# Silu and SSM-branch tiles: PSUM copied out by ScalarE, the product on GpSimd; y tiles loaded first in the GLU stage

## Chip, cores and metric

The kernel runs on one core of a Trainium2 chip. The metric is the device time of one execution in microseconds (us). Times and rows below come from the runs of the kernel before and from one execution of it that the hardware profiler recorded.

## What is computed

One step of a hybrid encoder layer (D_MODEL 1024) on two token streams: a prompt of 1024 tokens and a sample of 32 tokens with a cache of 512. Everything is fp32. Cut to what the change touches:

```python
h = rms_norm(x, g_norm) * (1.0 + scale) + shift
z = h @ w_in
u, zs, q, k, v, za, qi, ki, wi, gm = split(z)
ys, hr, hi = ssm_scan(u, ...)                 # 32 groups of 16 channels, 64 complex states
ys = gelu(ys)
ys = ys * sigmoid(ys @ w_glu + b_glu)
ys = ys * silu(zs)
o  = sparse_attention(q, k, v, top-k keys by relu(qi . ki) weighted with wi)
ya = o * silu(za)
g_s, g_a = split(gm)
merged = sigmoid(g_s) * (ys @ w_ps) + sigmoid(g_a) * (ya @ w_pa)
x_new = x + gate * (merged @ w_o)             # then a final rms_norm
```

Here silu(x) = x * sigmoid(x), and the kernel gets it as (1 + tanh(x/2)) * x with the factor 1/2 taken up elsewhere. The sigmoid of the gates is made from a tanh in the same way.

## The kernel before

The two streams are put side by side: NT = 1056 columns (1024 + 32), cut into three column groups of G3 = 352. Features lie on the 128 partitions.

Each fp32 product is three fp32r matmuls (`mm3`, lines 271 to 273): high weights by high data, high weights by low data, low weights by high data. So each weight tile is split into `wh`, a cast of `raw` (line 259 on ScalarE, line 263 in pieces on GpSimd), and `wl = raw - wh` (line 264). The data are split into names that end in H and L.

The dense products are jobs in one queue, `Z`: u and zs tiles, the indexer's ki and qi0 to qi3, glu0 to glu3, gates g0 to g15, K/V/Q of the heads, za0 to za3 (silu of za), m0 to m7 (`psjob`, ys @ w_ps). A job has three column groups. A group is 3 x kt matmuls of 352 columns (kt = 8 for inputs of 1024 features, 4 for 512) into one PSUM bank: pool "z" (tile `pz`) has two banks; while nothing else uses them, halves of two larger tiles (`pss`) serve as well. A function `ev(n, ps)` empties a bank. The weights of the next job are split, and those of the one after it loaded, while the first column group of a job runs. `heng` and `leng` name the engines that make `wh` and `wl`.

The stages in order: modulation, norm and u (to about 90 us); SSM chains with zs, gates and ki between them (to about 245); the GLU stage (to about 305); indexer scores (318 to 405); 32 bisection rounds for the top-k threshold on VectorE and ScalarE, with K/V/Q and gates on TensorE (to 555); the marks of the chosen keys on VectorE, with za0 to za3 on TensorE (555 to 602); attention in four head pairs (608 to 893), m0 to m7 beside the last pair (815 to 905); then the merge and the output. TensorE's, VectorE's and ScalarE's orders are written by hand in most stages, GpSimd's and SyncE's (the DMA queue) are set by the tile scheduler. Every engine works through its own queue in order.

Names in the steps: `yD` is the GELU'd SSM output in DRAM, stored from `Yq` (line 991); `yg` its four tiles loaded again (line 1124), split into `ygH` (ScalarE, line 70) and `ygL` (line 73), the data of the glu jobs. `zsD` and `ztD` hold zs and its tanh; `gate_tile` loads them as `z2`, `t2` and forms the silu factor on VectorE (line 1090), `gate_y` multiplies it by yg (line 1095). `qis` are the parts of qi that VectorE and ScalarE take from its banks (lines 1067 to 1070). `cki` is the cached indexer keys. `th` (buffers "sth") is a tanh of one column group, `zt` a silu tile on its way to DRAM, `tg` in `psjob` (in the trace `tgl`) the tanh of a gate tile loaded from DRAM, `m1` (in the trace `m`) its product with ys @ w_ps, which is read again in the merge after 906 us. `PH` and `PL` are the halves of the attention weights.

Of the kernel before, what the change touches and what calls it, by code (L numbers as in the profile page):

```python
# [12 lines left out]
ALU = mybir.AluOpType  # L13
# [29 lines left out]
C_U, C_ZS, C_Q, C_K, C_V, C_ZA, C_QI, C_KI, C_GM = 0, 512, 1024, 1536, 2048, 2560, 3072, 3584, 3656  # L43
# [15 lines left out]
def body(nc, tc, I, O, dbg=None):  # L59
    ctx = ExitStack()  # L60
    dbg = dbg or (lambda name, ap: None)
    I = {k: v for k, v in I.items()}
    te, ve, se, ge, sp = nc.tensor, nc.vector, nc.scalar, nc.gpsimd, nc.sync

    def f32(ap):
        return ap.bitcast(F32)

    def split(h, l, src, heng, leng):
        if heng is se:
            se.copy(h, src)  # L70
        else:
            heng.tensor_copy(h, src)
        leng.tensor_sub(l, src, f32(h))  # L73
# [14 lines left out]
    def ps_x(tag, bufs, w=512):  # L88
        t = phase[1].tile([128, w], F32, tag=tag, bufs=bufs, name="ps" + tag)
        return t  # L90
# [14 lines left out]
    def ps_s(n="pss"):  # L105
        return ps_x("s", 2, 1024)
# [15 lines left out]
    def load_rows(xt, g, r, n, eng):  # L122
# [3 lines left out]
        if k < n:  # L126
# [30 lines left out]
                            op0=ALU.add, op1=ALU.mult)  # L157
# [163 lines left out]
    now, ve = ve, Later(ve, todo)  # L321
# [149 lines left out]
    for k in range(7):  # L471
        n = 1 << k
# [39 lines left out]
    ve = now  # L512
# [29 lines left out]
    ns = lambda n: slice(n * G3, (n + 1) * G3)  # L542
# [145 lines left out]
    ztD = [dram.tile([128, NT], F32, name=f"ztD{q}") for q in range(4)]  # L688
    zaD = [dram.tile([128, NT], F32, name=f"zaD{q}") for q in range(4)]

    def silu_job(name, c0, dst, heng, leng, th_dst=None):

        def begin():
            zt = stg.tile([128, NT], F32, tag="stg", name="zt")
            zth = stg.tile([128, NT], F32, name="zth", tag="zth", bufs=1) if th_dst is not None else None

            def ev(n, ps):
                if th_dst is not None:
                    se.activation(zth[:, ns(n)], ps, AF.Tanh, scale=0.5)
                    se.copy(zt[:, ns(n)], ps)  # L700
                else:
                    th = stg.tile([128, G3], F32, tag="sth", name="th")
                    se.activation(th, ps, AF.Tanh, scale=0.5)
                    ve.scalar_tensor_tensor(zt[:, ns(n)], th, 1.0, ps, op0=ALU.add, op1=ALU.mult)
                if n == 2:
                    sp.dma_start(dst, zt)
                    if th_dst is not None:
                        sp.dma_start(th_dst, zth)
            return ev
        return Job(name, wcol(c0), begin, heng=heng, leng=leng)  # L710

    def gate_job(f, heng, leng):
        def begin():
            tg = stg.tile([128, NT], F32, tag="stg", name="tg")

            def ev(n, ps):
                se.activation(tg[:, ns(n)], ps, AF.Tanh, scale=0.5)  # L717
                if n == 2:
                    sp.dma_start(thD[f], tg)
            return ev  # L720
        return Job(f"g{f}", wcol(C_GM + 128 * f), begin, heng=heng, leng=leng)
# [53 lines left out]
    for t in START.split():  # L775
# [6 lines left out]
        else:  # L782
            n = t.rstrip("0123456789")
            STEP[n](*(int(c) for c in t[len(n):]))
        if t == "wl00":
            ssm_shifts()
    ssm_consts()
    sp.dma_start(uD[0], uP[0])
    sp.dma_start(uD[1], uP[1])
    Z.add(*(silu_job(f"zs{q}", C_ZS + 128 * q, zsD[q], se, ge, ztD[q]) for q in range(4)),  # L790
          *(gate_job(f, se, ve) for f in range(NS)))
    while todo:
# [265 lines left out]
    cki = kp.tile([128, 4, 2, 64], F32)  # L1058
    QS = {}

    def qijob(j):
        def begin():
            qs = QS[j] = [kp.tile([128, NT], F32R, name=f"qis{e}", bufs=2) for e in range(2)]

            def ev(n, ps):
                c = ns(n)
                se.copy(qs[0][0:64, c], ps[0:64])
                se.copy(qs[1][64:128, c], ps[64:128])
                ve.tensor_sub(qs[0][64:128, c], ps[0:64], f32(qs[0][0:64, c]))
                ve.tensor_sub(qs[1][0:64, c], ps[64:128], f32(qs[1][64:128, c]))  # L1070
            return ev
        return Job(f"qi{j}", wcol(C_QI + 128 * j), begin, heng=se, leng=ve)
# [7 lines left out]
    def tok(t):  # L1080
        return ((t[:, 0:1024].rearrange("p (c s) -> p c s", s=8), slice(0, 128)),
                (t[:, 1024:NT].rearrange("p (c s) -> p c s", s=8), slice(129, 133)))
# [3 lines left out]
    def gate_tile(q):  # L1086
        z2, t2 = (gp.tile([128, NT], F32, name=n, bufs=b) for n, b in (("z2", 2), ("t2", 1)))
        sp.dma_start(z2, zsD[q])
        sp.dma_start(t2, ztD[q])
        ve.scalar_tensor_tensor(z2, t2, 1.0, z2, op0=ALU.add, op1=ALU.mult)  # L1090
        Z2.append(z2)

    def gate_y(q):
        for v_, c in tok(Z2[q]):
            ve.tensor_mul(v_, v_, yg[q][:, c])

    def glu_job(q):
        def begin():
            z2 = Z2[q]

            def ev(n, ps):
                c = ns(n)
                th = stg.tile([128, G3], F32, tag="sth", name="th")
                se.activation(th, ps, AF.Tanh, scale=0.25, bias=bglu[:, q:q + 1])
                ve.scalar_tensor_tensor(z2[:, c], th, 1.0, z2[:, c], op0=ALU.add, op1=ALU.mult)
                yo = [gp.tile([128, G3], F32R, name=f"yo{h}", bufs=3) for h in range(2)]
                split(yo[0], yo[1], z2[:, c], se, ge)
                for h in range(2):
                    sp.dma_start(ysD[h][q][:, c], f32(yo[h]))
                if n == 2 and q < 2:  # L1110
                    gate_tile(q + 2)
                    gate_y(q + 2)
            return ev
        return Job(f"glu{q}", w_glu[:, 128 * q:128 * q + 128], begin, kt=4, heng=se, leng=ve,
                   rhs=lambda n, k: (ygH[k][:, ns(n)], ygL[k][:, ns(n)]))

    for q in range(2):
        gate_tile(q)
    ckd = I["cache_kidx"].rearrange("a b (k p) d -> p (a b k) d", p=128)
    for hf_ in range(2):  # L1120
        sp.dma_start(cki[:, :, hf_], ckd)
    for q in range(4):
        yg.append(gp.tile([128, 8, NCH], F32, name=f"yg{q}").rearrange("p s c -> p c s"))
        sp.dma_start(yg[q].rearrange("p c s -> p s c"), yD[q])
# [1 line left out]
            split(h_, l_, yg[q][:, c], se, (ge, ve)[(YS >> q) & 1])  # L1126
    w_glu = I["w_glu"].rearrange("o d e -> (o d) e")
    for q in range(2):
        gate_y(q)
    Z.add(*(glu_job(q) for q in range(4)), qijob(1), *(gate_job(f, se, ve) for f in range(NS, NI - 1)))  # L1130
    Z.add(qijob(2), qijob(3), gate_job(NI - 1, se, ve), hold=True)
    Z.until("glu3")
# [49 lines left out]
    for k in range(9):  # L1182
        n = 128 if k < 8 else 32
# [16 lines left out]
    for j in range(4):  # L1200
# [3 lines left out]
        for i in range(2, 9):  # L1204
            t0, m, k0, nk = (128 * i, 128, 0, 128 * (i + 1)) if i < 8 else (1024, 32, 1024, 544)
            for e in range(2):
                h = 2 * j + e
                ps = ps_s()
                for a in range(0, nk, 512):
                    b = min(nk, a + 512)  # L1210
# [7 lines left out]
                else:  # L1218
                    ve.scalar_tensor_tensor(sco[i][:m, :nk], rl[:m, :nk], w, sco[i][:m, :nk],  # L1219
                                            op0=ALU.mult, op1=ALU.add)  # L1220
# [150 lines left out]
    class Soft:  # L1371

        def products(self, m, nk, mask, lhsT, rhs, np_=0):
            self.m, self.nk, self.mask, self.np_ = m, nk, mask, np_
            self.P = at2.tile([128, 1024], F32, name="Sm", bufs=SM)
            self.S = []
            for a in range(0, nk, 512):
                c = slice(a, min(nk, a + 512))
                S = ps_x("s", 3)[:m, 0:c.stop - a]
                self.S.append((c, S))  # L1380
                for t, r in enumerate(rhs):
                    te.matmul(S, lhsT, r[:, c], start=t == 0, stop=t == len(rhs) - 1)  # L1382
# [172 lines left out]
    def q0_end():  # L1555
# [3 lines left out]
        X.heads()  # L1559
    X.qjob.end = q0_end  # L1560
    Z.add(X.kjob, X.vjob, X.qjob, *(gate_job(f, ge, ge) for f in range(NI, 16)),
          *(silu_job(f"za{q}", C_ZA + 128 * q, zaD[q], se, ge) for q in range(4)))
    m1, PB = [], []

    def ps_branch():
# [7 lines left out]
    def psjob(f):  # L1573
        def begin():
            m1.append(late["fin"].tile([128, NT], F32, name="m1", tag="mm", bufs=8))
            tg = stg.tile([128, NT], F32, name="tgl", tag="stg")
            sp.dma_start(tg, thD[f])

            def ev(n, ps):
                ve.scalar_tensor_tensor(m1[f][:, ns(n)], tg[:, ns(n)], 1.0, ps, op0=ALU.add, op1=ALU.mult)  # L1580
            return ev
        return Job(f"m{f}", I["w_ps"].rearrange("o d e -> (o d) e")[:, 128 * f:128 * f + 128], begin, kt=4,
                   heng=se, leng=ge, rhs=lambda n, k: (PB[0][k, n], PB[1][k, n]))
# [95 lines left out]
    for k in range(len(seq) + 3):  # L1679
        it = at(k)  # L1680
        if k in first:
            p, begin = first[k]
# [10 lines left out]
        f = FA[p][e_] + FF * (it.i + 1 if it else 5)  # L1693
# [77 lines left out]
    for f in range(8):  # L1771
        wh, wl = wsplit(w_pa[:, 128 * f:128 * f + 128], 4, 128)
        tg = stg.tile([128, NT], F32, name="tgl", tag="stg")
        sp.dma_start(tg, thD[8 + f])
        for n in range(3):
            ps = ps_x("m", 4)
# [63 lines left out]
    for rows in ((0, 1, 2), (8,), (3,), (4,), (5,), (6,), (LAST,)):  # L1840
        xts = {}
        for hcol in range(2):
            for i in rows:
                n = 128 if i < 8 else 32
# [5 lines left out]
                for b_, c in enumerate(cols):  # L1850
                    ps = products(i, n, hcol, c)
# [4 lines left out]
                    if len(cols) == 2 and b_ == 0:  # L1856
                        ve.tensor_scalar(ss2[:n, 0, i:i + 1], ss2[:n, 0, i:i + 1], ss2[:n, 1, i:i + 1], None,
                                         op0=ALU.add)
# [53 lines left out]
```

## Time and profile before

| | us |
|---|---|
| three runs | 1049.63, 1050.88, 1049.40 |
| median | 1049.63 |
| the profiled execution's own time | 1053.21 |
| its span in the profile | 1051.4 |
| TensorE matmul busy | 999.1 (95%) |
| VectorE busy | 768.1 (73%) |
| ScalarE busy | 542.0 (52%) |
| GpSimd busy | 250.5 (24%) |

PE is TensorE's matmuls, PEld its weight loads, DVE is VectorE, ACT ScalarE, POOL GpSimd, SP SyncE, which issues nearly all DMAs. [...] In a row of the timeline the brackets say how long the engine stood idle before it and what ended that.

### The profile page before, as it was taken

What the parts mean: (1) busy time and instruction counts of PE and PEld (TensorE: products, weight loads), DVE (VectorE), ACT (ScalarE), POOL (GpSimd) and SP (SyncE); (2) the same over time, 40 slices, a digit from 0 to 9 for tenths busy, and PEclk for the clock granted to TensorE, in tenths of its full rate; (3) what the DMA queues carried; (4) which work ended last, traced back from release to release, by engine and by line L of the source; (5) the groups of instructions that cost most, each with busy time, mean ns of one, the idle gap of its engine ahead of it and who ended that gap; (6) DMA issues with size and microseconds to landing.
All of it is one profiled execution on the core that took longest, in us unless ns stands there. A gap on an engine that the chain in (4) does not pass through costs nothing.

```text
span 1051.4 us, 17200 instructions
## 1 busy us (share of the span) xinstructions
PE 999.1 (95%) x6194; PEld 929.9 (88%) x6194; DVE 768.1 (73%) x1756; ACT 542.0 (52%) x1164; POOL 250.5 (24%) x467
## 2 busy tenths in 40 slices
PE   5899999999899999998998999999999999999997
PEld 3799999999788989998998998899898988998786
DVE  4569898994776879988889846756658776786534
ACT  3542345544545656768994346655566555443111
POOL 4102400000240013333313532333233131340000
PEclk9899999999899999998998999999999999999999
DMA  9922632328483222223232341242124632754311
GB/s 309 272 69 83 185 123 63 94 72 243 158 267 101 61 61 81 79 84 92 82 103 82 104 141 53 63 132 70 59 86 126 203 93 75 268 164 139 128 63 60
DMA packets 125329, 126.00 MB, mean 120 GB/s; under 512 B 14400, under 2 KB 104980, under 8 KB 125244
## 3 DMA queue, kind: packets, MB, share of 16 engines
q1 hardware_dynamic: 124864, 124.59, 38.4%
q8 instruction: 49, 0.80, 0.3%
q14 instruction: 36, 0.29, 0.1%
q10 hardware_dynamic: 220, 0.28, 0.1%
q0 software_dynamic: 160, 0.03, 0.0%
HBM read 87.81 MB, written 36.50 MB: 118 GB/s over the span
## 4 chain that ended last, share of the span: by engine, by line
PE 66%; DVE 11%; ACT 10%; issue 5%; DMA 5%; SPq 1%; POOL 1%; ACTq 0%; POOLq 0%; DVEq 0%
PE pz L271 10%; PE pz L272 10%; PE pz L273 10%; ACT junkb L1546 5%; PE pss L1382 3%; PE psm L1881 3%; PE psm L1882 3%; PE psm L1883 3%; DMA wm<-in_w_mod 2%; PE pss L271 2%; PE pss L273 2%; DVE junk L1548 2%; PE pt L1475 2%; PE pss L272 2%; PE pspo L1494 2%
## 5 line engine op out<-in xcount | busy, mean ns | idle before, releaser
L271 PE MATMUL pz<-hH,wh 128*128 128x352 f32 (+1 forms) x776 | 260.1, 335 | 0.3 <-DVE qis L1070 0.2
L273 PE MATMUL pz<-hH,wl 128*128 128x352 f32 (+1 forms) x776 | 250.7, 323 | 0.0
L272 PE MATMUL pz<-hL,wh 128*128 128x352 f32 (+1 forms) x776 | 250.7, 323 | 0.0
L264 POOL TENSOR_TENSOR wl<-raw,wh 128x256 fp32r<-128x256 f32 (+1 forms) x184 | 133.7, 754 | 118.6 <-ACT wh L259 118.3
L271 PEld LDWEIGHTS pz<-hH,wh 128*128 128x128 f32 (+1 forms) x776 | 145.0, 187 | 4.2 <-issue 0.8
L272 PEld LDWEIGHTS pz<-hL,wh 128*128 128x128 f32 (+1 forms) x776 | 145.1, 187 | 1.5
L273 PEld LDWEIGHTS pz<-hH,wl 128*128 128x128 f32 (+1 forms) x776 | 144.9, 187 | 0.4
L1546 ACT ACTIVATE junkb<-sco,thr 128x896 bf16<-128x896 f32 (+3 forms) x128 | 103.5, 809 | 30.8 <-DVE thr L1611 20.7
L271 PE MATMUL pss<-hH,wh 128*128 128x352 f32 x304 | 103.8, 341 | 9.9 <-ACT tg L717 6.4
L272 PE MATMUL pss<-hL,wh 128*128 128x352 f32 x304 | 101.5, 334 | 0.3 <-DVE hL L73 0.2
L273 PE MATMUL pss<-hH,wl 128*128 128x352 f32 x304 | 101.3, 333 | 0.4 <-POOL wl L264 0.4
L1548 DVE TENSOR_SCALAR_CACHE_REDUCE junk<-sco,thr 128x1024 bf16<-128x1024 f32 (+2 forms) x96 | 96.9, 1010 | 2.3
L263 POOL CAST wh<-raw 128x256 fp32r<-128x256 f32 x88 | 34.7, 434 | 185.1 <-PE pz L272 169.3
L271 PEld LDWEIGHTS pss<-hH,wh 128*128 128x128 f32 x304 | 59.9, 197 | 13.9 <-POOL wh L263 5.2
L1478 DVE TENSOR_TENSOR PL<-pt,PH 128x512 fp32r<-128x512 f32 (+2 forms) x96 | 50.4, 553 | 27.7 <-ACT PH L1477 26.6
L1477 ACT CAST PH<-pt 128x512 fp32r<-128x512 f32 (+2 forms) x96 | 43.0, 482 | 42.9 <-PE pt L1475 39.6
L272 PEld LDWEIGHTS pss<-hL,wh 128*128 128x128 f32 x304 | 60.0, 197 | 0.8 <-DVE hL L73 0.8
L273 PEld LDWEIGHTS pss<-hH,wl 128*128 128x128 f32 x304 | 59.7, 196 | 0.9 <-POOL wl L264 0.9
L1219 DVE SCALAR_TENSOR_TENSOR sco<-rl,wi,sco 128x384 f32<-128x384 f32 (+6 forms) x49 | 45.6, 936 | 15.9 <-ACT rl L1214 15.3
L1214 ACT ACTIVATE rl<-pss 128x384 f32<-128x384 f32 (+6 forms) x56 | 41.1, 738 | 29.8 <-PE pss L1212 26.0
L1395 ACT ACTIVATE Sm<-Sm,mx 128x128 f32<-128x128 f32 (+8 forms) x68 | 52.7, 775 | 7.0 <-DVE mx L1388 7.0
L1883 PE MATMUL psm<-o,mL 128*128 128x512 f32 (+1 forms) x136 | 51.7, 381 | 0.0
(410 smaller groups left out, 2246.6 us busy)
## 6 DMA issues: line engine op xcount, KB each, us to landing
raw<-in_w_in SPq DMA_DIRECT2D x44, 512.0 KB
thD<-tg SPq DMA_DIRECT2D x16, 528.0 KB
tgl<-thD SPq DMA_DIRECT2D x16, 528.0 KB
wm<-in_w_mod SPq DMA_DIRECT2D x8, 1024.0 KB
rraw<-in_w_mod SPq DMA_DIRECT2D x4, 1024.0 KB
kd<-kd SPq DMA_DIRECT2D x32, 128.0 KB
xo<-in_x_prompt SPq DMA_DIRECT2D x8, 512.0 KB
rawo<-in_w_o SPq DMA_DIRECT2D x8, 512.0 KB
```

The costliest lines, as they stand in the source:

```text
L264: leng.tensor_sub(wl[:, c], raw[:, c], f32(wh[:, c]))
L271: te.matmul(ps, wh, xh, start=first, stop=False)
L272: te.matmul(ps, wh, xl, start=False, stop=False)
L273: te.matmul(ps, wl, xh, start=False, stop=last)
L1214: se.activation(rl[:m, :nk], ps[:m, :nk], AF.Relu)
L1219: ve.scalar_tensor_tensor(sco[i][:m, :nk], rl[:m, :nk], w, sco[i][:m, :nk], op0=ALU.mult, op1=ALU.add)
L1395: se.activation(P, P, AF.Exp, scale=-1.0, bias=self.mx, accum_out=self.rs)
L1477: se.copy(PH[:, b0:b1_, oc], src)
L1478: ve.tensor_sub(PL[:, b0:b1_, oc], src, f32(PH[:, b0:b1_, oc]))
L1546: se.activation(junkb[:m, :nk], x[:m], AF.Sign, bias=t, accum_out=cnt[:m, k:k + 1])
L1548: ve.tensor_scalar(junk[:m, :nk], x[:m], t, None, op0=ALU.is_lt, op1=ALU.add, accum_out=cnt[:m, k:k + 1])
L1883: te.matmul(ps, ml, wh, start=False, stop=last)
```

## The change

Three edits. A silu job without a stored tanh (za0 to za3) no longer has VectorE form (th + 1) * ps from PSUM; ScalarE copies the bank into zt, GpSimd adds 1 to th and multiplies zt by it. The m jobs do the same with the loaded tanh. The weights of za0 are cast by GpSimd instead of ScalarE. And in the GLU stage the loads and splits of the four y tiles are written ahead of the silu factors and the cki loads.

```diff
+    def one_plus(t):
+        ge.tensor_scalar(t, t, 1.0, 1.0, op0=ALU.mult, op1=ALU.add)
+
     def silu_job(name, c0, dst, heng, leng, th_dst=None):
...
                     th = stg.tile([128, G3], F32, tag="sth", name="th")
                     se.activation(th, ps, AF.Tanh, scale=0.5)
-                    ve.scalar_tensor_tensor(zt[:, ns(n)], th, 1.0, ps, op0=ALU.add, op1=ALU.mult)
+                    se.copy(zt[:, ns(n)], ps)
+                    one_plus(th)
+                    ge.tensor_mul(zt[:, ns(n)], zt[:, ns(n)], th)
...
-    for q in range(2):
-        gate_tile(q)
-    ckd = I["cache_kidx"].rearrange("a b (k p) d -> p (a b k) d", p=128)
-    for hf_ in range(2):
-        sp.dma_start(cki[:, :, hf_], ckd)
     for q in range(4):
         yg.append(gp.tile([128, 8, NCH], F32, name=f"yg{q}").rearrange("p s c -> p c s"))
         sp.dma_start(yg[q].rearrange("p c s -> p s c"), yD[q])
...
     for q in range(2):
+        gate_tile(q)
         gate_y(q)
+    ckd = I["cache_kidx"].rearrange("a b (k p) d -> p (a b k) d", p=128)
+    for hf_ in range(2):
+        sp.dma_start(cki[:, :, hf_], ckd)
...
-          *(silu_job(f"za{q}", C_ZA + 128 * q, zaD[q], se, ge) for q in range(4)))
+          *(silu_job(f"za{q}", C_ZA + 128 * q, zaD[q], se if q else ge, ge) for q in range(4)))
...
             def ev(n, ps):
-                ve.scalar_tensor_tensor(m1[f][:, ns(n)], tg[:, ns(n)], 1.0, ps, op0=ALU.add, op1=ALU.mult)
+                se.copy(m1[f][:, ns(n)], ps)
+                one_plus(tg[:, ns(n)])
+                ge.tensor_mul(m1[f][:, ns(n)], m1[f][:, ns(n)], tg[:, ns(n)])
```

SyncE's queue at the start of the GLU stage, before: the first row is the store of the fourth y tile; z and t are the loads of `gate_tile` from zsD and ztD.

```order
L991 DMA yD_1418<-Yq 128x8x133
L1088 DMA z_2724<-zsD_217 128x1056
L1089 DMA t_2725<-ztD_221 128x1056
L1088 DMA z_2729<-zsD_218 128x1056
L1121 DMA cki<-in_cache_kidx 128x4x64 x2
L1124 DMA yg_2736<-yD_1415 128x1064
L1124 DMA yg_2742<-yD_1416 128x1064
L1124 DMA yg_2748<-yD_1417 128x1064
L1124 DMA yg_2754<-yD_1418 128x1064
```

The same place after the change (lines shift by 5 to 12):

```order
L996 DMA yD_1418<-Yq 128x8x133
L1124 DMA yg_2724<-yD_1415 128x1064
L1124 DMA yg_2730<-yD_1416 128x1064
L1124 DMA yg_2736<-yD_1417 128x1064
L1124 DMA yg_2742<-yD_1418 128x1064
L1093 DMA z_2748<-zsD_217 128x1056
L1094 DMA t_2749<-ztD_221 128x1056
L1093 DMA z_2755<-zsD_218 128x1056
L1133 DMA cki<-in_cache_kidx 128x4x64 x2
```

The four loads of the y tiles moved ahead of z, t, z and cki. VectorE's queue at the same place, before: `ygL` are the low halves of the y tiles, the rows of lines 1069 and 1070 empty a bank of qi0.

```order
L1090 SCALAR_TENSOR_TENSOR z_2724<-t_2725,z_2724 128x1056
L1069 TENSOR_TENSOR qis_2856<-pz,qis_2856 64x352
L1070 TENSOR_TENSOR qis_2857<-pz,qis_2857 64x352
L1095 TENSOR_TENSOR z_2724<-z_2724,yg_2736 128x1024
L1095 TENSOR_TENSOR z_2724<-z_2724,yg_2736 128x32
L73 TENSOR_TENSOR ygL_2720<-yg_2736,ygH_2716 128x1024
L73 TENSOR_TENSOR ygL_2720<-yg_2736,ygH_2716 128x32
L1069 TENSOR_TENSOR qis_2856<-pz,qis_2856 64x352
L1070 TENSOR_TENSOR qis_2857<-pz,qis_2857 64x352
L73 TENSOR_TENSOR ygL_2721<-yg_2742,ygH_2717 128x1024
L73 TENSOR_TENSOR ygL_2721<-yg_2742,ygH_2717 128x32
```

After the change:

```order
L73 TENSOR_TENSOR ygL_2720<-yg_2724,ygH_2716 128x1024
L73 TENSOR_TENSOR ygL_2720<-yg_2724,ygH_2716 128x32
L264 TENSOR_TENSOR wl<-raw,wh 128x512
L73 TENSOR_TENSOR ygL_2721<-yg_2730,ygH_2717 128x1024
L73 TENSOR_TENSOR ygL_2721<-yg_2730,ygH_2717 128x32
L73 TENSOR_TENSOR ygL_2722<-yg_2736,ygH_2718 128x1024
L73 TENSOR_TENSOR ygL_2722<-yg_2736,ygH_2718 128x32
L1074 TENSOR_TENSOR qis_2856<-pz,qis_2856 64x352
L1075 TENSOR_TENSOR qis_2857<-pz,qis_2857 64x352
L73 TENSOR_TENSOR ygL_2723<-yg_2742,ygH_2719 128x1024
L73 TENSOR_TENSOR ygL_2723<-yg_2742,ygH_2719 128x32
L1095 SCALAR_TENSOR_TENSOR z_2748<-t_2749,z_2748 128x1056
```

The first evacuation of qi0 (lines 1069 and 1070 before, 1074 and 1075 after) moved from ahead of all low halves to behind three of them. GpSimd's queue from the last gates to the start of the attention, before: pieces of weight casts (line 263) and low parts (line 264).

```order
L263 CAST wh<-raw 128x256 x4
L264 TENSOR_TENSOR wl<-raw,wh 128x256 x20
L263 CAST wh<-raw 128x256 x4
L1480 MEMSET PH 128x128
L1481 MEMSET PL 128x128
```

After the change, up to the weights of za3: line 692 is `one_plus`, line 709 the product.

```order
L263 CAST wh<-raw 128x256 x4
L264 TENSOR_TENSOR wl<-raw,wh 128x256 x8
L692 TENSOR_SCALAR th<-th 128x352
L709 TENSOR_TENSOR zt<-zt,th 128x352
L692 TENSOR_SCALAR th<-th 128x352
L709 TENSOR_TENSOR zt<-zt,th 128x352
L264 TENSOR_TENSOR wl<-raw,wh 128x256 x4
L692 TENSOR_SCALAR th<-th 128x352 x2
L709 TENSOR_TENSOR zt<-zt,th 128x352 x2
L692 TENSOR_SCALAR th<-th 128x352
L709 TENSOR_TENSOR zt<-zt,th 128x352
L264 TENSOR_TENSOR wl<-raw,wh 128x256 x4
```

za0's cast is now GpSimd's (the first row), its low part and za1's are the eight pieces behind it, za2's four pieces stand behind two evacuations, and za3's behind three more.

## Rows read from the trace of the kernel before

**Rows 1.** First part of the page: busy time of the engines over the whole span.

```profile
PE 999.1 (95%) x6194; PEld 929.9 (88%) x6194; DVE 768.1 (73%) x1756; ACT 542.0 (52%) x1164; POOL 250.5 (24%) x467
```

**Rows 2.** Five stretches: length, busy us (x instructions) by engine, PEclk, DMA share, GB/s.

```profile
254.00:264.00 10.00, 9.75 (x61) 9.45 (x60) 7.07 (x8) 5.68 (x7) 0.00 (x0) 1.00 1.02 358
263.70:272.40 8.70, 3.91 (x14) 2.41 (x13) 8.65 (x10) 7.08 (x10) 0.00 (x0) 0.76 0.04 15
272.40:278.50 6.10, 6.10 (x21) 6.10 (x22) 5.03 (x7) 1.53 (x3) 2.55 (x2) 0.50 0.59 191
558.30:565.20 6.90, 6.47 (x21) 6.02 (x22) 6.76 (x7) 2.86 (x6) 5.09 (x5) 0.51 0.26 93
815.00:906.00 91.00, 86.62 (x572) 80.78 (x571) 63.73 (x171) 48.34 (x106) 22.36 (x54) 1.00 0.49 156
```

**Rows 3.** Timeline of SyncE's queue, 245 to 258 us: start, us, DMA issues.

```profile
253.18 3.36 SPq L1124 DMA_DIRECT2D yg<-yD  x4
```

**Rows 4.** Waits of SyncE's queue, 230 to 310 us: total, times, longest us.

```profile
SPq L1121 <- DMA yD<-Yq: 3.5, 1, 3.5
```

**Rows 5.** Waits of TensorE, 263 to 273 us, the start of glu0.

```profile
PE pz L272 <- DVE ygL L73: 3.2, 3, 1.3
PE pz L271 <- ACT ygH L70: 1.0, 1, 1.0
```

**Rows 6.** Timeline of ScalarE, 250 to 275 us, the first y tile.

```profile
259.15 2.28 ACT L70 CAST ygH<-yg 128x1024 fp32r<-128x1024 f32 x2 [2.14 <-DMA yg<-yD]
```

**Rows 7.** Timeline of VectorE, 250 to 283 us.

```profile
254.64 1.26 DVE L1090 SCALAR_TENSOR_TENSOR z<-t,z 128x1056 f32<-128x1056 f32 x1 [1.20 <-DMA t<-ztD]
259.22 2.21 DVE L1095 TENSOR_TENSOR z<-z,yg 128x1024 f32<-128x1024 f32 x2 [1.12 <-DMA yg<-yD]
264.06 0.53 DVE L1070 TENSOR_TENSOR qis<-pz,qis 64x352 fp32r<-64x352 f32 x1
264.62 6.21 DVE L73 TENSOR_TENSOR ygL<-yg,ygH 128x1024 fp32r<-128x1024 f32 x6
```

**Rows 8.** Timeline of TensorE, 553 to 567 us, za0's first matmuls.

```profile
558.27 0.61 PE L271 MATMUL pss<-hH,wh 128*128 128x352 f32 x1 [2.63 <-ACT wh L259]
...
559.61 0.66 PE L273 MATMUL pss<-hH,wl 128*128 128x352 f32 x1 [0.43 <-POOL wl L264]
```

**Rows 9.** Timeline of ScalarE, 552 to 606 us: weight casts of za0 and za2.

```profile
557.19 1.03 ACT L259 CAST wh<-raw 128x1024 fp32r<-128x1024 f32 x1
...
576.46 1.03 ACT L259 CAST wh<-raw 128x1024 fp32r<-128x1024 f32 x1
```

**Rows 10.** Timeline of GpSimd, 525 to 606 us: weight casts and low parts.

```profile
532.51 1.44 POOL L263 CAST wh<-raw 128x256 fp32r<-128x256 f32 x4 [8.49 <-PE pz L272]
533.91 2.84 POOL L264 TENSOR_TENSOR wl<-raw,wh 128x256 fp32r<-128x256 f32 x4
558.30 5.07 POOL L264 TENSOR_TENSOR wl<-raw,wh 128x256 fp32r<-128x256 f32 x4 [21.55 <-ACT wh L259]
...
577.57 5.34 POOL L264 TENSOR_TENSOR wl<-raw,wh 128x256 fp32r<-128x256 f32 x4 [8.17 <-ACT wh L259]
```

**Rows 11.** Waits of all engines, 815 to 906 us: the row of the m jobs.

```profile
PE pz L271 <- DVE m L1580: 4.1, 5, 1.4
```

**Rows 12.** Tiles m, zt and yo: count, duration ns min/median/max, first and last start.

```profile
L1580 DVE SCALAR_TENSOR_TENSOR m<-tgl,pz x24: 500/512/522, 819.4 to 904.8; 128x352 f32<-128x352 f32 x24
L700 ACT COPY zt<-pz x12: 446/447/463, 100.2 to 150.1; 128x352 f32<-128x352 f32 x12
L73 POOL TENSOR_TENSOR yo<-z,yo x12: 936/1090/2157, 274.8 to 304.2; 128x352 fp32r<-128x352 f32 x12
```

**Rows 13.** Timelines of GpSimd and VectorE, 838 to 884 us: one form twice.

```profile
841.48 0.87 DVE L1404 TENSOR_SCALAR Sm<-Sm,rs 128x384 f32<-128x384 f32 x1
...
876.75 0.42 DVE L1404 TENSOR_SCALAR Sm<-Sm,rs 128x384 f32<-128x384 f32 x1
...
840.84 1.29 POOL L73 TENSOR_TENSOR kL<-kd,kH 128x512 fp32r<-128x512 f32 x1 [2.72 <-DVE kH L72]
```

## The prediction

> **What bounds the kernel now.** I first read the page's busy line: TensorE's matmuls fill 999.1 of 1051.4 us [rows 1], in one stream whose order is written by hand. So no time comes from making VectorE, ScalarE or GpSimd less busy as such. What can be won is the 52 us in which TensorE stands, and the stretches in which it runs at the lower of its two clock levels. I then cut the span around the places that the diff touches and read granted clock and matmul count for each [rows 2]. [...] At full clock a 352-column matmul comes every 10.00/61 = 0.16 us. [...] The m jobs' stretch (815 to 906) is at 1.00 throughout.
>
> Then the waits at these places. GLU: the load order on the queue [rows 3, 4], and glu0's matmuls, which wait four times for the halves of the y tiles, 4.2 us in all [rows 5]. za: the first matmul waits 2.63 us for ScalarE's weight cast and the third 0.43 us for GpSimd's part [rows 8]. m: five waits, 4.1 us in all, for VectorE to empty the PSUM bank [rows 11].
>
> **The change part by part.**
>
> *GLU order.* Before, the four yg loads stand behind two cki loads, which wait 3.5 us for the last yD store to land [rows 3, 4]; ScalarE reaches ygH0 only at 259.15, after 2.14 us for the load [rows 6]. After it, yg0 to yg2 take the places of z0, t0, z1, about 6 us sooner, and only yg3 waits for the store. The splits no longer hold glu0's matmuls: the four waits and the low clock behind them go. At full clock glu0's 36 matmuls are 36 x 0.16 = 5.8 us, and they now take from 264 to 279.6, so some 10 us is at stake. But the splits now stand *ahead* of qi0's evacuations on both engines. A y tile costs ScalarE 2.28 us [rows 6] and VectorE 6.21/3 = 2.1 us [rows 7]. With ygH0 from 252.8, ygH1 and ygH2 follow to 260.5, the qis casts to 261.4; VectorE's ygL2 ends near 262.7 and its qis pair (2 x 0.53) near 263.8. The pool "z" has two banks, so qi0's third column group, which starts at 259.7 now, must wait until about 263.9: a new stall of 4 us inside qi0. Its 24 remaining matmuls then end at 267.8 at full clock, or at 270.9 at 0.29 us each, if the clock falls as it does behind the 2.63 us wait of the za jobs. And glu0's second group needs qi0's last bank, which VectorE empties behind ygL3 (2.1), z0's gate (1.26), a qis pair (1.06), z0 times yg0 (2.21), a weight's low part (about 1.0: half a y tile's columns) and its own pair (1.06): 263.8 + 8.7 = 272.5. From there 24 matmuls: 276.4 at full clock, 279.5 at half. Against 279.6 that is a gain of 0.1 to 3.2; I take **-2**.
>
> *za0's weight cast to GpSimd.* Before, the cast (1.03 us) stands at 557.19 on ScalarE behind a counting round [rows 9], so za0 starts 2.63 us late, waits another 0.43 us, and the 6.90 us window behind it holds 21 matmuls, that is 21 x 0.16 = 3.4 us of work at full clock [rows 2, 8]. Lost: 2.63 + 6.90 - 3.4 = 6.1 us. GpSimd is idle for 21.55 us ahead of 558.30 [rows 10]; its cast and low part for one job cost 1.44 + 2.84 us there, and the raw weights have been loaded long before. So za0's weights are ready near 549, and the matmuls run on from 555.6. Recovered: 6.1.
>
> *za evacuations.* Twelve of VectorE's steps of 0.51 us become a ScalarE copy (0.45), a GpSimd one_plus and a GpSimd product. No row has one_plus. Below, it costs what a cast of 256 columns does, 0.36 us [rows 10], so 0.5 for 352; above, the longest product, 2.16. I take 0.9, nearer to the cast, since it too reads one tensor. The product has a near row, yo: 0.94 to 2.16, mean of the twelve about 1.3 [rows 12]. Together 2.2 us, between 1.4 and 4.3. What hides them: nothing reads zt until its store, but GpSimd is in order, and za2's low part stands behind the evacuations e0 and e1. Before, za2's weight cast starts at 576.46 on ScalarE right behind e1's tanh [rows 9]. After, e1's copy ends near 577.0, its two GpSimd steps near 578.8, and the first of four wl pieces (5.34/4 = 1.33 us each in this stretch [rows 10]) near 580.1. TensorE, now earlier, comes to za2 at 555.6 + 2 x 72 x 0.16 = 578.7 and needs the piece 0.3 us later: 1.1 us late. Each further piece covers six matmuls (0.96 us), so it loses 0.37, three times: 1.1. That makes 2.2; since the pieces vary down to 0.71 us, which would leave only the first 0.5, I take 1.7. With pieces of 0.71 us and evacuations of 1.4 there is no stall; with 4.3 each of the two is 2.1 later, some 5.9 in all. za3's part stands behind e2 to e4: 578.8 + 4 x 1.33 + 3 x 2.2 + 1.33 = 592.0 for its first piece, and TensorE needs it at 590.1 + 1.7 + 0.3 = 592.1: no stall. Net **-4.4**, between -6.1 and 0. VectorE is relieved of 6 us while it makes the marks, which is not on TensorE's path.
>
> *m evacuations.* The 24 VectorE steps of 0.51 us [rows 12] become ScalarE copies of 0.45, which frees the bank 0.06 us sooner and, mainly, does not stand behind VectorE's softmax work: the five waits are 4.1 us [rows 11]. ScalarE has its own queue of casts and exponentials, so not all goes. I take half, **-2**, between -4.1 and a loss of 3 if weights come late behind the GpSimd products. GpSimd's load there is 22.4 of 91 us [rows 2]; 24 x 2.2 makes it 75 of 91. The products themselves are not urgent: m is read only after 906.
>
> A row shows that GpSimd and VectorE can hinder each other: one 128x384 scaling on VectorE takes 0.87 us at 841.48, while GpSimd runs a subtract, and the same form 0.42 us at 876.75, where GpSimd is idle at first [rows 13]. If each of the 24 evacuations costs VectorE one such 0.45 us, that is 10.8 us against the 12.3 us that it is relieved of, so the sum stays. [...]
>
> **Sum.** -2 - 4.4 - 2 = -8.4 on the profiled execution's own 1053.21 us (1.8 us more than its span), so 1044.8. That execution is 3.6 us above the runs' median, 1049.63; I carry the difference to the median: 1041.2, say **1041**.
>
> **The rivals.**
>
> *R1: the gains are eaten.* GLU's stall only moves into qi0 with its low clock (0.1), za2's stall takes 2.7 and brings a low-clock stretch (3.4 us, as at za0), so za keeps nothing, and m gains 0 to 1: 1048.5 to 1049.5. For it: both new stalls come out of the order itself, and the clock fell behind a 2.63 us wait. Against it: behind the m waits of up to 1.4 us it did not fall [rows 2, 11], and za2's stall is near that size.
>
> *R2: GpSimd becomes the bound in the m stage (slower).* Its queue holds the weights' low parts of m1 to m7 and of the next stage between the products. With p us per evacuation its load is 22.4 + 24p. It passes 91 us at p = 2.9, and eats the whole sum and 2 us more at 22.4 + 24p = 91 + 10.5, so p = 3.3. At p = 4.3 (both steps at the longest yo) the load is 125.6, 34.6 over: 1049.6 - 6.4 + 34.6 = 1078; at 3.5 it is 106.4, 1059. For it: yo has a row of 2.16 us and the wl pieces vary from 0.71 to 1.33 us with what runs beside them. Against it: yo's middle is 1.09.
>
> *R3: only za gains* (GLU 0.1, m 0): 1045.1. Or less of za as well, up to 1047.5.
>
> **How the numbers follow.** The forecast (1036 to 1044.5) has 0.60, R3 with other part gains (1044.5 to 1047.5) 0.18, R1 0.12, R2 0.10. Below the forecast's middle lies the case that za and m give all (6.1 + 4.1) and GLU 3.2: 1036.2. About 0.2% (2.1 us) is what a measurement of this kernel can tell from no change. So faster than 1047.5 has 0.78, within 0.2% 0.12, slower 0.10. The range runs from 1036 to 1048, leaving out R2 and most of R1.
>
> **What the changed profile would show.** GLU: ygH0 near 253, no waits of glu0's matmuls for ygH or ygL, a new wait of 3 to 5 us in qi0 for VectorE's qis, glu0 ending 2 us sooner. za: GpSimd's casts before 550, no wait at 555.6, full clock there, and a 1 to 2 us wait at za2 for GpSimd's wl; one_plus near 0.9 us. m: waits on PSUM now on ScalarE's copy, about half as long; GpSimd near 70 of 91 us busy. I am wrong if the clock falls behind the stall in qi0 *and* behind za2's, if GpSimd's steps cost 3 us or more per evacuation, or if the qis evacuations are not what glu0 waits for.

## The result, and the profile after

The changed kernel takes 1054.61 us (median of five runs, 1053.07 to 1057.85). Against the kernel before, the ratio is 1.0051, with a 95% interval of 1.0032 to 1.0071: 5.3 us slower, between 3.4 and 7.5. The forecast was 1041, with a range of 1036 to 1048 and a chance of 0.10 for slower; the time lies above the range.

First the page's busy line of the kernel after, which answers to [rows 1].

```profile
PE 993.5 (94%) x6194; PEld 925.8 (88%) x6194; DVE 767.2 (73%) x1720; ACT 552.5 (52%) x1199; POOL 305.1 (29%) x543
```

TensorE is busy 5.6 us less than before and the span is 1.3 us longer: it stands more. VectorE is relieved by only 0.9 us, though 36 steps of 0.51 us (18.4 us) were taken from it. GpSimd has 54.6 us more.

The two profiled executions can't be set side by side without one correction. The next rows are stretches of the kernel after (columns as in [rows 2]; PEclk there is the granted TensorE clock as a share of full speed, 0.98 over the whole execution before).

```profile
0.00:50.00 50.00, 37.38 (x275) 28.24 (x276) 28.18 (x99) 25.65 (x47) 15.07 (x40) 1.00 1.03 301
259.70:266.50 6.80, 6.68 (x25) 6.71 (x26) 6.51 (x7) 0.75 (x2) 0.00 (x0) 0.55 0.25 80
555.00:565.00 10.00, 10.00 (x64) 10.00 (x63) 9.75 (x11) 2.96 (x7) 3.08 (x3) 1.00 0.13 54
606.00:614.00 8.00, 7.28 (x35) 7.28 (x36) 1.76 (x9) 2.92 (x9) 7.83 (x14) 0.72 0.66 201
815.00:906.00 91.00, 86.52 (x567) 79.96 (x567) 58.89 (x151) 56.93 (x131) 54.69 (x98) 1.00 0.47 153
```

In the first 50 us the clock is 1.00 here; in the profiled execution of the kernel before it is 0.90 there, which costs that one some 4 us ahead of anything that the change touches (the first matmul into `pz` starts at 72.68 there and at 68.46 here). So a span longer by 1.3 us means some 5.3 us lost behind it, and that is what the medians say. The place is found by following the same matmul in both traces; the list gives its start after minus its start before (us), where a stage begins or ends; a single number in brackets is the time in the kernel before.

```
qi0 begins its last column group's wait      -3.5
glu0 ends (278.93 before, 273.06 after)      -5.9
glu3, second group (293.71, 290.99)          -2.7
end of the GLU stage (306)                   -3.5
counting rounds near their end (551)         -3.0
za0's groups behind the start (571)          -8.7
za3 near its end (607)                       -7.4
attention running (612)                      +0.5
m jobs begin (814)                           +0.8
m7 near its end (896)                        -0.3
merge running (910)                          +1.3
```

Three stages gain at the places that the change aims at, and each gives all of it back, or more, at its end or at the start of the next. The largest loss is 7.9 us between za3 and the attention. The waits of TensorE over the whole span show where (total, times, longest us):

```profile
PE pss L1386 <- ACT zt L707: 5.9, 1, 5.9
...
PE pz L271 <- DVE qis L1075: 4.2, 2, 3.4
...
PE pz L271 <- ACT m L1584: 2.3, 4, 0.9
...
PE pss L273 <- POOL wl L264: 0.8, 2, 0.5
```

The 2.63 us wait for za0's cast [rows 8] and the waits for ygL and ygH [rows 5] are gone, the m wait is 2.3 instead of 4.1 us [rows 11]. New are 5.9 us at line 1386, the attention's first score matmul, and 3.4 of the 4.2 us for qis. (The waits for `tg`, 6.4 us in all before and 8.5 after, are left aside: in the traces of the runs below they go up to 11.2 (e11), and no edit touches the gate jobs.) TensorE at the start of the attention:

```profile
600.46 0.32 PE L273 MATMUL pz<-hH,wl 128*128 128x352 f32 x1
606.72 0.47 PE L1386 MATMUL pss<-kH,qs 128*128 128x128 f32 x1 [5.94 <-ACT zt L707]
...
607.61 0.49 PE L272 MATMUL pz<-hL,wh 128*128 128x352 f32 x1
607.90 0.49 PE L273 MATMUL pz<-hH,wl 128*128 128x352 f32 x1
```

za3's last matmul starts at 600.46 and the next thing at 606.72, and what follows runs at the lower clock level at first (a matmul every 0.29 us, as from 607.61 to 607.90; 0.72 granted over 606 to 614). ScalarE and GpSimd there:

```profile
600.13 0.47 ACT L706 ACTIVATE th<-pss 128x352 f32<-128x352 f32 x1 [1.22 <-POOL zt L709]
...
605.86 0.46 ACT L706 ACTIVATE th<-pss 128x352 f32<-128x352 f32 x1 [4.92 <-POOL zt L709]
606.22 0.45 ACT L707 COPY zt<-pss 128x352 f32<-128x352 f32 x1
```

```profile
600.33 1.43 POOL L263 CAST wh<-raw 128x256 fp32r<-128x256 f32 x4
601.73 0.49 POOL L692 TENSOR_SCALAR th<-th 128x352 f32<-128x352 f32 x1
602.17 2.77 POOL L264 TENSOR_TENSOR wl<-raw,wh 128x256 fp32r<-128x256 f32 x4
604.90 0.93 POOL L709 TENSOR_TENSOR zt<-zt,th 128x352 f32<-128x352 f32 x1
```

Read backwards: the bank was freed by the copy at 606.22; that stands behind a tanh that began at 605.86, after 4.92 us of waiting for GpSimd; the buffer it waited for (`th` has two) was freed by the product at 604.90; and that product stands in GpSimd's queue behind four wl pieces (602.17, 2.77 us) for the attention's first weights, though its operands were there from 602.2 on. Its one_plus, at 601.73, had itself stood behind the four casts of those weights (1.43 us).

### The profile page after: what moved, and what is told of

Same layout as the page of the kernel before. It is cut to its first block, busy times and chain, and to the rows that moved or that the text cites. A ratio compares the mean times of both kernels' runs of the same rounds, so it can differ in the third digit from the quotient of the medians.

```text
span 1052.7 us, 17310 instructions
## 1 busy us (share of the span) xinstructions
PE 993.5 (94%) x6194; PEld 925.8 (88%) x6194; DVE 767.2 (73%) x1720; ACT 552.5 (52%) x1199; POOL 305.1 (29%) x543
## 4 chain that ended last, share of the span: by engine, by line
PE 61%; DVE 13%; ACT 11%; DMA 7%; issue 4%; POOL 2%; SPq 1%; POOLq 0%; ACTq 0%; DVEq 0%
PE pz L271 10%; PE pz L272 9%; PE pz L273 9%; ACT junkb L1550 7%; PE pss L1386 3%; PE psm L1887 3%; PE psm L1888 3%; PE psm L1889 3%; DMA wm<-in_w_mod 2%; DVE junk L1552 2%; PE pt L1479 2%; PE pspo L1498 2%; PE pss L1216 2%; PE pss L1215 2%; PE psm L272 1%
## 5 line engine op out<-in xcount | busy, mean ns | idle before, releaser
L1392 DVE CUSTOM_DVE_ANT_0 Sm<-pss,mb 128x512 f32<-128x512 f32 (+4 forms) x68 | 40.1, 590 | 23.7 <-PE pss L1386 23.0
```

What stands on the lines that cost most here:

```text
L1392: ve.tensor_tensor_reduce(self.P[:m, c], S, self.mask[:m, c], -0.125, 3.0e38 if a == 0 else mx[:m, 0:1], op0=ALU.add, op1=ALU.min, accum_o ...
```

## The experiments

Each was timed in five rounds against the kernel before on the same chip; ratios carry their 95% interval. Medians of the kernel before were 1049.93 (e1 to e4), 1048.69 (e5 to e8), 1049.18 (e9 to e11) and 1049.13 (e12).

**The parts alone (e1 to e4).** e1 has the GLU hunks of the diff, e2 the `se if q else ge` of za0, e3 the evacuation of `silu_job`, e4 that of `psjob`; nothing else differs from the kernel before.

e1: 

> The GLU reorder alone. Theory A (the loss sits in the za stage, where ScalarE's last tanh waits for a th buffer that GpSimd frees late): this edit alone is near zero, 0 to +1.5 us, because glu0's stalls (4.8 us and the low clock) are replaced by one of 3.4 us in qi0 with a low clock of its own, and glu2 waits longer for its bank. Rival B (the reorder itself is a good part of the loss): +2 us or more.

e2: 

> Only za0's weight cast moves to GpSimd. Theory A: -3 to -5 us: the 2.63 and 0.43 us waits and the low clock at za0 go, VectorE still empties the za banks, and at the attention's first matmul a wait of at most 2 us appears, since the marks on VectorE end no sooner. Rival C (za's end is set by the marks on VectorE whatever TensorE does): 0 to -1 us, with all of the gain given back in a wait at the attention's start.

e3: 

> Only the za banks are emptied by ScalarE's copy with the product on GpSimd; za0's cast stays on ScalarE, so za ends near 608 as before. Theory A: -1 to +2 us, since GpSimd's late th buffers (freed near 606) are hardly waited for when TensorE itself comes 6 us later. Rival D (GpSimd's new work hinders VectorE's marks and the weights wherever it is put): +3 us or more.

e4: 

> Only the m banks are emptied by ScalarE's copy with the product on GpSimd. Theory A: -1.5 to +1 us: the waits of TensorE for the bank fall from 4.1 to about 2.3 us, and part of that is given back behind 900 us, where VectorE's split of b takes 1.93 instead of 1.23 us beside GpSimd. Rival D (GpSimd's work beside VectorE costs more than it frees): +2 us or more.

| | median us | ratio | interval |
|---|---|---|---|
| e1 GLU order | 1048.63 | 0.9991 | 0.9974 to 1.0009 |
| e2 za0's cast | 1046.03 | 0.9976 | 0.9962 to 0.9990 |
| e3 za evacuation | 1054.21 | 1.0045 | 1.0031 to 1.0058 |
| e4 m evacuation | 1051.16 | 1.0023 | 1.0008 to 1.0037 |

By the ratios that is -0.9, -2.5, +4.7 and +2.4 us, in sum +3.7, within the interval of the whole. The cast gains, by its middle less than the 3 to 5 us expected and more than rival C's 0 to 1; both moves of products to GpSimd lose, each alone. That is more than theory A expected of e3 (-1 to +2) and e4 (-1.5 to +1), and in the range of rival D. e3's profiled execution took 1061.62 us, 7.4 above the median of its runs, so its whole time says little. But its own waits from 545 to 625 us show the same chain as the changed kernel:

```profile
PE pss L271 <- ACT wh L259: 4.1, 1, 4.1
PE pss L1387 <- ACT zt L707: 3.0, 1, 3.0
```

The 3.0 us wait for the za bank is there though za0 starts late. The reason that A gave for its absence was wrong: the chain does not stay where it was while TensorE comes later. ScalarE's last tanhs stand behind its own counts of the marks, of which the last waits 2.28 us for VectorE in e3 (2.27 in the changed kernel), and GpSimd's products stand behind the tanhs. So the chain moves with the marks, and in e3 the tanh waits 4.96 us for its buffer. From the end of za3 to the running attention e3's matmuls lose 4.8 us against the kernel before, most of its +4.7 and more than its wait, since the clock falls there too (0.87 granted over 608 to 616 us and 0.92 over 616 to 624, after 1.00 over 600 to 608). In e2, where VectorE empties the banks, TensorE shows this:

```profile
552.01 0.40 PE L271 MATMUL pss<-hH,wh 128*128 128x352 f32 x1 [0.72 <-ACT tg L717]
...
600.65 0.33 PE L1382 MATMUL pss<-kH,qs 128*128 128x128 f32 x1 [1.83 <-DVE zt L704]
```

za0 starts without a wait for the weights, and the attention waits 1.83 us, as A expected (at most 2). VectorE makes the last evacuations behind the last mark (597.58); that much of rival C holds.

**Buffer or load (e5).** The changed kernel with one edit:

```diff
-                    th = stg.tile([128, G3], F32, tag="sth", name="th")
-                    se.activation(th, ps, AF.Tanh, scale=0.5)
                     se.copy(zt[:, ns(n)], ps)
+                    th = stg.tile([128, G3], F32, tag="sth", name="th")
+                    se.activation(th, zt[:, ns(n)], AF.Tanh, scale=0.5)
```

> The changed kernel, but in za's evacuation the copy out of the bank comes first and the tanh is taken from the copy in SBUF, so that no bank waits for a th buffer that GpSimd has to free. Theory A (ScalarE stands before its last tanh until GpSimd frees th, and so the attention's first matmul waits 5.9 us for a bank and then runs at the lower clock): 4 to 8 us faster than the changed kernel, that is 1047 to 1051. Rival D (GpSimd's work beside VectorE is the cost, not the buffers): within 2 us of the changed kernel's 1054.6.

Measured: 1048.47 us, ratio 0.9997 (0.9980 to 1.0015) to the kernel before; against the changed kernel's 1.0051 that is 5.7 us back. GpSimd's and ScalarE's work are the same. ScalarE in e5:

```profile
598.62 0.50 ACT L707 ACTIVATE th<-zt 128x352 f32<-128x352 f32 x1 [0.71 <-POOL zt L709]
599.03 0.43 ACT L705 COPY zt<-pss 128x352 f32<-128x352 f32 x1
604.40 0.50 ACT L707 ACTIVATE th<-zt 128x352 f32<-128x352 f32 x1 [4.94 <-POOL zt L709]
```

and TensorE:

```profile
599.94 0.32 PE L273 MATMUL pz<-hH,wl 128*128 128x352 f32 x1
600.10 0.22 PE L1386 MATMUL pss<-kH,qs 128*128 128x128 f32 x1
```

The tanh still waits 4.94 us for GpSimd, at the same point of the program. But the bank's copy stands ahead of it, at 599.03, and the attention's first matmul follows za3 with no wait. So the loss at the attention is the bank held behind a buffer. GpSimd's work as such costs less: TensorE waits 0.6 us for wl at the attention's start and 1.6 us in za2. A third `th` buffer was not tried.

**Without GpSimd's products (e6, e7), and the parts that gain (e8).** e6 is the changed kernel with VectorE's old line in `silu_job`. e7 keeps both copies on ScalarE, with products such as

```diff
-                one_plus(tg[:, ns(n)])
-                ge.tensor_mul(m1[f][:, ns(n)], m1[f][:, ns(n)], tg[:, ns(n)])
+                ve.scalar_tensor_tensor(m1[f][:, ns(n)], tg[:, ns(n)], 1.0, m1[f][:, ns(n)], op0=ALU.add, op1=ALU.mult)
```

e8 is e1 and e2 together.

e6: 

> The changed kernel with VectorE emptying the za banks as before; za0's cast on GpSimd, the GLU order and the m edit stay. If the single edits add up: 1049.9 - 0.9 - 2.5 + 2.4 = 1049. If the m edit's loss comes only when the rest is as before (it is a wait at the merge), less: 1047. If the za evacuation isn't what costs: 1053 or more.

e7: 

> The changed kernel, but both products are made by VectorE in one step from the copies in SBUF; GpSimd makes none, ScalarE still copies the banks out. Theory A at za: VectorE frees the th buffers as fast as before, so the wait at the attention's start falls to about 2 us and the time to 1047 to 1050. For m: if the loss there comes from GpSimd's products it goes too (1046 to 1048); if it comes from TensorE arriving sooner at a merge whose inputs aren't loaded, it stays (1048 to 1050). Rival: if ScalarE's added copies are the cost, no better than 1053.

e8: 

> Only the two parts that gained alone: the GLU order and za0's cast on GpSimd; za and m banks emptied by VectorE as before. If they add: -0.9 - 2.5 = -3.4 us against the kernel before, about 1046.5. If the earlier GLU end is given back in the counting stage as well as in the other runs: -1.5 to -2.5.

e6 is 1048.24 (0.9996, 0.9984 to 1.0008), e7 1048.18 (0.9998, 0.9987 to 1.0009), e8 1046.61 (0.9977, 0.9968 to 0.9987). e6 fits that the parts add (-1.0 by their sum, -0.4 measured): taking the za evacuation out gives back what it cost. In e7 both copies stay on ScalarE and the tanh stays ahead of the copy, and with the products on VectorE the loss goes as well. So ScalarE's copies are not the cost, and the loss at the attention needs both GpSimd's late product and the bank held behind it. In e7's trace the attention's first matmul still waits 2.6 us for ScalarE's copy. e8 gains 2.4 us; the sum of e1 and e2 is 3.4, from ratios that are each uncertain by 1.5 to 2 us. It is faster than both kernels.

**za mended, m left alone (e9, e10).** e9 is e8 with e5's copy first and GpSimd's product, e10 the same with one VectorE step for the product.

e9: 

> GLU order, za0's cast, and za's evacuation with the copy first and the product on GpSimd; the m banks are emptied by VectorE as before. It is the run with the copy first (1048.5) without the m edit. If the m edit costs 2.4 us here as it does alone: 1046. If the m edit's cost was only a wait that comes and goes with the run: 1048 to 1049.

e10: 

> As the last, but the product is one VectorE step from SBUF. No GpSimd work is added to the za stage, and no bank waits for a th buffer. Theory A: the 1.8 us wait at the attention's start that stays when VectorE empties the banks goes, so about 1045; if VectorE's steps delay its marks as before and the attention's first softmax waits for those, 1046 to 1047.

e9 is 1046.69 (0.9969, 0.9948 to 0.9990), e10 1048.60 (0.9989, 0.9970 to 1.0008). e9 is faster than both kernels and about e8, so with the copy first GpSimd's za products neither gain nor lose measurably; its difference from e5 (0.9997) fits the m edit's +2.4. e10 missed both of its values, 1045 and 1046 to 1047: the wait at the attention's start did not go.

```profile
601.14 0.50 ACT L704 ACTIVATE th<-zt 128x352 f32<-128x352 f32 x1 [0.72 <-DVE zt L705]
...
602.03 0.33 PE L1382 MATMUL pss<-kH,qs 128*128 128x128 f32 x1 [2.02 <-ACT zt L702]
```

The copy that frees the bank stands ahead of its own tanh, but behind that of the group before, which waits for a buffer; VectorE frees that one behind its last mark (600.18). e10's interval overlaps e9's, so which engine should make the product stays open.

**What costs in the m edit (e11, e12).** e11 is the m edit alone with the product on VectorE, as in e7's diff. e12 splits it: GpSimd for `f < 5`, VectorE for m5 to m7.

e11: 

> The m edit alone, with the copy on ScalarE but the product as one VectorE step from SBUF; GpSimd gets nothing. If the m edit's loss (+2.4 us) comes from TensorE reaching the merge 1 to 2 us sooner than its inputs and from the copies in ScalarE's queue, it stays: +1.5 to +2.5. If it comes from GpSimd's products beside VectorE and in front of the merge's weights: 0 or a gain of 1.

e12: 

> The m edit alone; GpSimd makes the products of m0 to m4, VectorE those of m5 to m7 from SBUF. Theory E (GpSimd's late products hold the last tgl buffers, so that the merge's first loads stand closer behind tgl on the queue, and slow VectorE's split of b): the loss of the m edit (+2.4 us) goes, to between -1 and +1, and TensorE's wait for b at the merge is under 0.6 us (1.3 with all products on GpSimd). Rival F (GpSimd's products cost all through the m stage): +1 to +2, and the wait at the merge stays.

e11 is 1048.90 (0.9998, 0.9981 to 1.0016), e12 1049.51 (0.9991, 0.9978 to 1.0005). e11 came out as expected for a loss by GpSimd's products, though its interval alone overlaps e4's (1.0008 to 1.0037). e12's lies below it, by little: the products of the last three jobs make the loss, and with those of the first five alone on GpSimd none is seen. That is as theory E expected; rival F's +1 to +2 lies outside the interval (-2.3 to +0.5). The waits of TensorE from 815 to 912 us, in e4:

```profile
PE pz L271 <- ACT m L1583: 2.2, 4, 0.9
PE psm L271 <- ACT b L70: 1.3, 1, 1.3
```

and in e12:

```profile
PE pz L271 <- ACT m L1583: 2.1, 4, 0.9
```

The bank's wait is the same 2.1 to 2.2 us in both. Of the two only e4 has the 1.3 us wait for b at the merge. (The other kernels with all m products on GpSimd have it too, at different lengths: 1.7 us in e6, 0.7 in e5, 0.2 in the changed kernel.) Behind it the clock falls (window of e4):

```profile
900.90:904.60 3.70, 3.70 (x14) 3.70 (x15) 3.62 (x5) 2.15 (x6) 3.70 (x5) 0.55 1.10 268
```

14 matmuls in 3.70 us. The DMA queue shows what stands ahead of the merge's first load, `src`; e4:

```profile
889.22 0.32 SPq L1580 DMA_DIRECT2D tgl<-thD  x1
...
890.58 0.38 SPq L1738 DMA_DIRECT2D src<-yaD  x1
```

and e12:

```profile
887.26 0.32 SPq L1580 DMA_DIRECT2D tgl<-thD  x1
...
889.92 0.38 SPq L1741 DMA_DIRECT2D src<-yaD  x1
```

ScalarE's first split of src, in e4 and then in e12:

```profile
898.53 1.05 ACT L70 CAST b<-src 128x1024 fp32r<-128x1024 f32 x1 [3.56 <-DMA src<-yaD]
```

```profile
896.32 1.05 ACT L70 CAST b<-src 128x1024 fp32r<-128x1024 f32 x1 [1.54 <-DMA src<-yaD]
```

In e4 the last tgl load (528 KB) goes out 1.4 us ahead of src, in e12 2.7, in the kernel before 3.1. A tgl load needs the buffer that the product two jobs earlier frees. From the issue of src to ScalarE's split, which waits for it, it is 7.95 us in e4, 6.40 in e12 and 6.87 in the kernel before. That the nearer load delays src fits these rows, and e6's (1.4 and 8.29), but the changed kernel has 1.5 and only 6.68. It was not tried by itself, so why the late products cost stays open beyond their place.

## Why the prediction was wrong

**za evacuations: the step that failed.** It said "What hides them: nothing reads zt until its store, but GpSimd is in order, and za2's low part stands behind the evacuations". It looked for who waits for GpSimd's queue and found only the weights. ScalarE waits for it too: `th` has two buffers, so each tanh needs the product two column groups back, and the copy that frees the bank is written behind the tanh. From there the chain is GpSimd, ScalarE, bank, TensorE. The list of GpSimd's queue shown ahead of the prediction stops at za3's weights; the place that costs lies just behind it. The term was -4.4 for cast and evacuation together, with a worst case of 0; e2 and e3 measure -2.5 and +4.7. e5 shows the cause: it takes the bank out of this chain, leaves GpSimd's work as it was, and 5.7 us come back.

The prices in the term were too high, not too low, which is why R2 was not the way in which it went wrong. GpSimd's groups from 565 to 616 us (xcount, then busy us and mean ns):

```profile
L709 POOL TENSOR_TENSOR zt<-zt,th 128x352 f32<-128x352 f32 x12 | 13.8, 1151 | 0.7
L692 POOL TENSOR_SCALAR th<-th 128x352 f32<-128x352 f32 x12 | 7.3, 613 | 8.4 <-ACT th L706 8.4
```

and from 815 to 906 us:

```profile
L1586 POOL TENSOR_TENSOR m<-m,tgl 128x352 f32<-128x352 f32 x22 | 21.1, 967 | 11.1 <-ACT m L1584 8.9 <-DVE mx L1392 2.2
L692 POOL TENSOR_SCALAR tgl<-tgl 128x352 f32<-128x352 f32 x21 | 10.5, 525 | 15.4 <-DMA tgl<-thD 15.4
```

An evacuation costs 1.76 us at za and 1.49 at m, against 2.2 taken. GpSimd is busy 54.69 of 91 us in the m stretch, against 75 taken and 91 for R2. That rival gave "slower" its chance of 0.10; the kernel is slower by another way. A busy share far from its limit said nothing of the one place where a wl group stands ahead of a product that a bank waits for.

**za0's cast: mechanism right.** GpSimd makes the weights by 545.3, and za0's first matmul:

```profile
541.03 1.44 POOL L263 CAST wh<-raw 128x256 fp32r<-128x256 f32 x4 [7.29 <-PE pz L272]
542.42 2.84 POOL L264 TENSOR_TENSOR wl<-raw,wh 128x256 fp32r<-128x256 f32 x4
...
553.08 0.40 PE L271 MATMUL pss<-hH,wh 128*128 128x352 f32 x1 [0.44 <-ACT tg L722]
```

waits 0.44 us for a bank instead of 2.63 for the cast; the clock over 555 to 565 is 1.00. The following matmuls gain 5.7 us on the kernel before, where the term of 6.1 was worked out. Alone the cast keeps 2.5 of that by e2's runs: in e2's trace 5.5 us are won behind za0's start, 0.5 are lost within za and 2.1 at the attention's start, where it waits 1.8 us for VectorE's last evacuation. The term had no such end; that VectorE's marks are "not on TensorE's path" does not hold there. za2's wl wait, put at 1.7 us, is 0.8 for two waits in all, and the matmuls lose 1.4 us there.

**GLU order: right to the end of glu0.** TensorE:

```profile
259.82 0.63 PE L271 MATMUL pz<-hH,wh 128*128 128x352 f32 x1 [3.41 <-DVE qis L1075]
...
269.30 0.40 PE L271 MATMUL pz<-ygH,wh 128*128 128x352 f32 x1 [0.74 <-DVE qis L1075]
...
290.99 0.43 PE L271 MATMUL pz<-ygH,wh 128*128 128x352 f32 x1 [2.75 <-ACT th L1109]
```

The stall in qi0 is 3.41 us where 4 was worked out, and the clock does fall (0.55 over 259.7 to 266.5, with a matmul every 0.29 us from 260.25 to 265.24; the 0.29 us worked with is 6.10 us by 21 matmuls at a clock of 0.50 [rows 2]). glu0's second group starts at 269.30, that is 272.8 with the 3.5 us by which this execution is ahead; 272.5 was worked out. glu0 ends 2.4 us sooner, measured from the stage's start, where 2 was forecast. What was not followed is glu3: its second group waits 2.75 us for a tanh, against 1.09 us before, and the stage ends with nothing won in this trace. Why that tanh is later was not followed. e1 measures -0.9 (-2.7 to +0.9): both the forecast's -2 and the 0.1 of R1 and R3 lie in its interval.

**m evacuations.** The wait fell by 1.8 us, where half of 4.1 was taken: that size was right. m7's matmuls are 1.1 us ahead of where the m jobs began, then the merge gives it back: in e4 with its wait and clock, in the changed kernel with 0.9 us for VectorE's split of b among it. The term left out the next stage's inputs. With the last three products off GpSimd (e11, e12) the wait is as short, 2.1 to 2.2 us, and no gain is shown: -0.2 and -0.9, with -2 at the end of or inside both intervals. The bound "a loss of 3" was for late weights, which isn't what happened.

**VectorE's relief.** The sum held that GpSimd's work beside VectorE might cost about what it relieves. In the marks it costs more. The first `le` and the last `mb`, before and then after:

```profile
555.29 0.75 DVE L1618 TENSOR_SCALAR le<-sco,thr 128x1024 bf16<-128x1024 f32 x1
...
601.05 0.43 DVE L1627 TENSOR_TENSOR mb<-le,eq 32x544 bf16<-32x544 bf16 x1
```

```profile
553.03 0.76 DVE L1624 TENSOR_SCALAR le<-sco,thr 128x1024 bf16<-128x1024 f32 x1
...
599.32 1.07 DVE L1633 TENSOR_TENSOR mb<-le,eq 32x544 bf16<-32x544 bf16 x1
```

The marks take 47.4 us (553.03 to 600.39), 46.2 before, though seven of VectorE's twelve 0.51 us steps lay in between then. One row of VectorE beside one of GpSimd in the changed kernel:

```profile
572.14 0.90 DVE L1650 TENSOR_TENSOR keep<-cnt,nse 128x2 int32<-128x2 f32 x1
...
571.62 1.39 POOL L709 TENSOR_TENSOR zt<-zt,th 128x352 f32<-128x352 f32 x1
```

A step on two columns, 0.16 us in the kernel before (at 577.04, with GpSimd idle), takes 0.90 and ends within 0.03 us of the end of GpSimd's product (571.62 + 1.39 = 573.01). The marks' `mb` step:

```profile
L1633 DVE TENSOR_TENSOR mb<-le,eq x7: 424/978/1066, 558.2 to 599.3; 128x1024 bf16<-128x1024 bf16 x1, 128x768 bf16<-128x768 bf16 x1, 128x512 bf16<-128x512 bf16 x1, 128x896 bf16<-128x896 bf16 x1
```

has a middle of 0.98 us, before 0.63. What holds the one beside the other no run shows. Over the whole span VectorE's gain is about nothing (0.9 us), and GpSimd's two steps cost 1.76 and 1.49 us an evacuation, below the 2.2 taken and far from the upper 4.3.

## What to carry to other kernels

When an engine takes over the last step of an evacuation, follow its buffers back as well as forward: with two buffers and a queue worked through in order ahead of it (here four wl pieces, 2.77 us), the step that "nothing waits for" decides when the bank comes free. Put the copy that frees a bank ahead of whatever can wait; it still stands behind what waits in the group before it, as in e10 (2.02 us at the attention's first matmul). And read a stage's gain at its end and at the start of the next: here three stages won 1 to 6 us and gave all of it back there.

## What the runs showed of the hardware

GpSimd's `one_plus` on 128x352 fp32, for which there was no row, costs 0.53 us beside the attention's last pair and 0.61 from 565 to 616 us, beside the marks for the most part; that is about half of its product (0.97 and 1.15 us). In the kernel before, waits of up to 1.4 us left the clock at 1.00 in the m jobs [rows 2, 11]; with 1.3 us in e4, 3.4 us in qi0 and 5.9 us at the attention it fell, to 0.55, 0.55 and 0.72 over the stretches shown. A wait of 1.8 us at the attention's start left it at 1.00 over 600 to 606 us in e2; one of 1.9 us there was followed by 0.72 over the same stretch in e6. So the length of the one stall does not tell whether it falls.
